# A decoder layer's opening: x and the first weights on two DMA queues, x a second time by rows, one raw buffer set

## The chip, the cores and the metric

The kernel runs on one core of a Trainium2 chip. The metric is the device time of one execution in microseconds, from the first instruction to the last. TensorE multiplies matrices, VectorE (DVE in the profile), ScalarE (ACT) and GpSimd (POOL) work on rows of 128 partitions, and SyncE (SP) issues DMA transfers, which 16 DMA engines carry out. Each engine takes its own instructions strictly in order, and waits for others by semaphores. So an instruction that waits also holds up everything behind it on its engine.

## What the kernel computes

One layer of a decoder with 256 tokens of 1024 channels. Cut to its outline:

```python
h = rmsnorm(x, norm1_g)
proj = h @ w_in                          # 13 groups of columns: kv_c, kv_s, kv_w, q_a, gates, q_b, k_b, v_b ...
q_a, k_s, k_w, q_b, k_b = rope(rmsnorm per head)
y_a = nsa_mixer(...)                     # compressed, selected and window attention, gated
y_b = dilated_mixer(...)
mixed = sigmoid(g_ma) * (y_a @ w_o_a) + sigmoid(g_mb) * (y_b @ w_o_b)
x = x + mixed @ w_out
x = x + square(relu(rmsnorm(x, norm2_g) @ w_up)) @ w_down
```

All arithmetic is float32. The kernel holds each factor of a dense product as two parts, hi (x rounded to the float32r type) and lo (x - hi), and forms hi hi + lo hi + hi lo.

## The kernel before, in words

**Weights.** A list of pieces of [128 partitions, 768 columns] (840 for the four pieces of kv_w) is gone through in the order of use. `load_to` issues the load of a piece into a buffer `raw` (L160 to L164). `split_to` makes the hi part by a ScalarE cast (`wh`, L180) and the lo part by a subtraction (`wl`, L183), on VectorE mostly and on GpSimd for each third piece from the sixth on. `raw` has two buffer sets: one of five for 768 columns, and another (`rawg`) for kv_w alone. A load must wait until the piece that held its buffer has been split.

**The opening.** x lies transposed in `xT`, loaded in four parts that alternate with the four pieces of kv_c. `scale_x` (L242) multiplies by the norm's gain and makes the two parts of h, one on ScalarE (L243), the other on VectorE (L244). The division by the rms is put off to the products' outputs: `proj` (L277) scales each output row by `rs` when it copies it out of the accumulator (`y`, L302). `setup` (L252) works `rs` out: squares on ScalarE (`sx`), three additions on GpSimd, four one-column products on TensorE, then a power of -0.5 on GpSimd (L265). After it come the rotation tables `ropeg`, ten multiplications on GpSimd (L270) that need the loads `rope` and `gr`, and one for the compressed keys (L274).

**What follows.** kv_c's outputs are transposed on TensorE (`tp`, L378) and put into `kvT`; `make_blk` adds position terms on GpSimd (`b32`, L394, four additions), casts on ScalarE (`blk`, L398) and subtracts on VectorE (L399). The projections kv_s, kv_w and q_a run on TensorE in the meantime, then the compression (`hacc`).

**The order.** The kernel's own planner (`Order`) sets products between tasks; after it, a scheduler places each engine's instructions by its own estimate of when they are ready. Eight DMAs can be on their way: the ninth waits for the first, and so on. Any change at the beginning can therefore move instructions far behind it.

Of the kernel before, what the change touches and what calls it, by code (L numbers as in the profile page):

```python
# [11 lines left out]
F32 = mybir.dt.float32  # L12
# [7 lines left out]
S = 256  # L20
# [11 lines left out]
# Steps of tensor-engine time between the stages of a task, and numbers of buffers.  # L32
D = {"qk": 1.0, "sm": 4, "pv": 0.6, "dqk": 3, "dsm": 4, "rope": 8, "turn": 0.3, "kvc": 0.8, "cz": 1, "ch": 1, "ck": 6,
     "most": 3, "warm": 10, "kneed": "nsa4", "pool_lo": 3, "ahead": 5, "extra": 18, "xm": 5, "xn": 3,
# [70 lines left out]
def hybrid_layer(ctx: ExitStack, tc: tile.TileContext, A, out):  # L105
# [50 lines left out]
    def load_to(n):  # L156
        while len(raws) < min(n, len(pieces)):
            src = pieces[len(raws)]
            n = src.shape[1]
            raw = raw_p.tile([128, n], F32, name="raw", tag="raw" if n <= PIECE else "rawg")  # L160
            if len(raws) < 4:
                q = len(raws)
                nc.sync.dma_start(xT[:, 2 * q:2 * q + 2], A["xT"][:, 2 * q:2 * q + 2])
            nc.sync.dma_start(raw[:, :src.shape[1]], src)  # L164
            raws.append(raw)

    def split_to(n):
        most = min(n, len(pieces))
        while len(parts) < most:
# [10 lines left out]
            nc.scalar.copy(hi[:, :m], src)  # L180
# [14 lines left out]
    def cell():  # L195
        """The next [128, 128] block of the stream of blocks."""
# [7 lines left out]
    ident = const.tile([128, 128], F32, name="ident")  # L204
    nc.sync.dma_start(ident, A["ident"])
    g12 = const.tile([128, 16], F32, name="g12")
    nc.sync.dma_start(g12, A["g12"])
    xT = once([128, 8, S], F32, "xT")
    load_to(4)
# [24 lines left out]
    # keep the tensor engine's clock up while the first loads arrive  # L234
# [4 lines left out]
    # hidden state (times its gain, not yet over its rms) in two parts  # L239
    hT = [once([128, 8, S], F32R, f"hT{i}") for i in range(2)]  # L240

    def scale_x(k):  # L242
        nc.scalar.activation(hT[0][:, k], xT[:, k], AF.Copy, scale=g12[:, k:k + 1])  # L243
        nc.vector.scalar_tensor_tensor(hT[1][:, k], xT[:, k], g12[:, k:k + 1], f(hT[0][:, k]),  # L244
                                       op0=OP.mult, op1=OP.subtract)

# [1 line left out]
    rs = const.tile([128, NT], F32, name="rs")  # L248
    idr = const.tile([128, 128], F32R, name="idr")
    ropeg = {}  # L250

    def setup():  # L252
        sx = [once([128, 2, S], F32, f"sx{i}") for i in range(4)]
        for i in range(4):
            nc.scalar.activation(sx[i], xT[:, 2 * i:2 * i + 2], AF.Square, scale=1.0 / 32.0)
            if i:
                nc.gpsimd.tensor_add(sx[0], sx[0], sx[i])
        pt = tp_bank()
        for t in range(NT):
            for k in range(2):  # L260
                nc.tensor.matmul(pt[:, t:t + 1], sx[0][:, k, t * 128:(t + 1) * 128], ones[:, 0:1],
                                 start=k == 0, stop=k == 1)
        ss = const.tile([128, NT], F32, name="ss")
        nc.vector.tensor_scalar(ss, pt[:, 0:NT], EPS, None, op0=OP.add)
        nc.gpsimd.tensor_tensor(rs, ss, nhalf[:, 0:NT], op=OP.pow)  # L265
# [769 lines left out]
```

## Time and profile before

| | us |
|---|---|
| median of three runs | 474.08 (473.75 to 474.11) |
| span of the profiled execution | 474.4 |
| TensorE busy | 452.3 (95%) |
| VectorE busy | 351.9 (74%) |
| ScalarE busy | 295.0 (62%) |
| GpSimd busy | 209.0 (44%) |

The profiled execution's span lies 0.3 us above the median of the timed runs; the profile shows no time of its own outside the span. TensorE's share of 95% is an average: nearly all of its idle time lies in the first 77 us and in four short places later. A row of a timeline gives start and duration in us, engine, line, operation, the tiles written and read with their shapes, how many were merged into the row, and in brackets the idle time before it and what ended it.

### The profile page before, as it was taken

How to read it: one execution, taken by the hardware profiler on the slowest of the kernel's cores; microseconds unless marked ns; L12 is line 12 of the kernel's file. 1: busy time of each engine (PE TensorE's matmuls, PEld its weight loads, DVE VectorE, ACT ScalarE, POOL GpSimd, SP SyncE). 2: the span in 40 equal slices, each digit the busy share in tenths (PEclk: the TensorE clock that was granted, in tenths of full speed). 3: DMA queues.
4: the chain of work that ended last, by engine and by line, in shares of the span. 5: the costliest groups of instructions: out<-in, count | busy, mean ns of one | idle time of the engine just before them, and what ended most of it. 6: DMA issues, size and time to landing. Idle time of an engine off the chain costs nothing.

```text
span 474.4 us, 9304 instructions
## 1 busy us (share of the span) xinstructions
PE 452.3 (95%) x3472; PEld 436.4 (92%) x3474; DVE 351.9 (74%) x572; ACT 295.0 (62%) x637; POOL 209.0 (44%) x203
## 2 busy tenths in 40 slices
PE   7997897999899999999999899999999999999996
PEld 6896777999798898989999899999999999999996
DVE  3959998989988999998557979956556555555450
ACT  5747678487867897858697454665656643433430
POOL 2797775779587782813043519523333310000000
PEclk8999899999899999999999999999999999999999
DMA  7973557563343144234336574777666767767720
GB/s 246 356 232 101 161 170 249 152 193 101 99 140 129 34 134 134 77 103 123 102 96 188 182 225 133 205 199 194 180 192 178 195 194 203 193 205 197 196 87 11
DMA packets 29630, 76.93 MB, mean 162 GB/s; under 512 B 3809, under 2 KB 5265, under 8 KB 29457
## 3 DMA queue, kind: packets, MB, share of 16 engines
q1 hardware_dynamic: 29584, 76.34, 54.5%
q8 instruction: 27, 0.44, 0.4%
q14 instruction: 19, 0.15, 0.1%
HBM read 75.28 MB, written 1.05 MB: 161 GB/s over the span
## 4 chain that ended last, share of the span: by engine, by line
PE 79%; DVE 10%; issue 4%; DMA 3%; ACT 2%; SPq 1%; POOL 0%; DVEq 0%; ACTq 0%; POOLq 0%
PE acc L745 18%; PE acc L746 18%; PE acc L744 18%; PE acc L295 4%; PE acc L296 4%; PE acc L294 4%; DVE wl L183 3%; PE tp L511 2%; DMA raw<-in_kv_c 2%; DMA gr<-in_gr 2%; PE tp L335 1%; PE dsp L693 1%; PE sp L552 1%; DVE t L329 1%; DVE h L873 1%
## 5 line engine op out<-in xcount | busy, mean ns | idle before, releaser
L183 DVE TENSOR_TENSOR wl<-raw,wh 128x768 fp32r<-128x768 f32 (+2 forms) x154 | 160.7, 1047 | 70.5 <-ACT wh L180 69.8
L180 ACT CAST wh<-raw 128x768 fp32r<-128x768 f32 (+2 forms) x183 | 152.1, 841 | 77.8 <-PE acc L745 66.2
L183 POOL TENSOR_TENSOR wl<-raw,wh 128x768 fp32r<-128x768 f32 (+1 forms) x29 | 56.2, 1937 | 62.5 <-ACT wh L180 35.8
L745 PE MATMUL acc<-h,wh 128*128 128x256 f32 x256 | 71.8, 281 | 0.7 <-DVE h L873 0.6
L745 PE MATMUL acc<-u,wh 128*128 128x256 f32 x256 | 71.6, 280 | 0.0
L746 PE MATMUL acc<-u,wl 128*128 128x256 f32 x256 | 71.6, 280 | 0.0
L744 PE MATMUL acc<-u,wh 128*128 128x256 f32 x256 | 71.6, 279 | 0.0
L746 PE MATMUL acc<-h,wl 128*128 128x256 f32 x256 | 71.3, 279 | 0.0
L744 PE MATMUL acc<-h,wh 128*128 128x256 f32 x256 | 71.3, 280 | 0.0
L295 PE MATMUL acc<-wl,hT 128*128 128x384 f32 (+1 forms) x176 | 63.0, 358 | 5.3 <-POOL wl L183 3.2
L294 PE MATMUL acc<-wh,hT 128*128 128x384 f32 (+1 forms) x176 | 60.3, 355 | 2.7 <-ACT wh L180 2.6
L296 PE MATMUL acc<-wh,hT 128*128 128x384 f32 (+1 forms) x176 | 61.1, 350 | 0.0
L911 POOL TENSOR_TENSOR r<-r 128x256 f32<-128x256 f32 x32 | 31.7, 992 | 54.1 <-ACT r L910 54.1
L745 PEld LDWEIGHTS acc<-h,wh 128*128 128x128 f32 x256 | 48.2, 188 | 1.2 <-DVE h L873 1.1
L746 PEld LDWEIGHTS acc<-u,wl 128*128 128x128 f32 x256 | 48.2, 188 | 0.0
L745 PEld LDWEIGHTS acc<-u,wh 128*128 128x128 f32 x256 | 48.2, 188 | 0.0
L744 PEld LDWEIGHTS acc<-u,wh 128*128 128x128 f32 x256 | 48.2, 188 | 0.0
L746 PEld LDWEIGHTS acc<-h,wl 128*128 128x128 f32 x256 | 48.1, 188 | 0.0
L744 PEld LDWEIGHTS acc<-h,wh 128*128 128x128 f32 x256 | 48.0, 188 | 0.0
L295 PEld LDWEIGHTS acc<-wl,hT 128*128 128x128 f32 x176 | 34.7, 197 | 7.3 <-POOL wl L183 3.7
L294 PEld LDWEIGHTS acc<-wh,hT 128*128 128x128 f32 x176 | 33.6, 194 | 4.1 <-ACT wh L180 3.5
L746 PE MATMUL acc<-hT,wl 128*128 128x256 f32 x128 | 37.0, 289 | 0.0
(195 smaller groups left out, 1094.7 us busy)
## 6 DMA issues: line engine op xcount, KB each, us to landing
raw<-in_cells SPq DMA_DIRECT2D x128, 384.0 KB, 3.4
raw<-in_cw SPq DMA_DIRECT2D x10, 384.0 KB, 3.7
raw<-in_q_a SPq DMA_DIRECT2D x8, 384.0 KB, 3.2
raw<-in_q_b SPq DMA_DIRECT2D x8, 384.0 KB, 3.6
raw<-in_k_b SPq DMA_DIRECT2D x8, 384.0 KB, 3.1
raw<-in_v_b SPq DMA_DIRECT2D x8, 384.0 KB, 3.2
raw<-in_kv_w SPq DMA_DIRECT2D x4, 420.0 KB, 8.3
raw<-in_kv_c SPq DMA_DIRECT2D x4, 384.0 KB, 7.0
```

Of the source, the lines that this page charges most:

```text
L180: nc.scalar.copy(hi[:, :m], src)
L183: eng.tensor_sub(lo[:, :m], src, f(hi[:, :m]))
L294: nc.tensor.matmul(o, hT[0][:, k, ts], hi[:, c], start=k == 0, stop=False)
L295: nc.tensor.matmul(o, hT[0][:, k, ts], lo[:, c], start=False, stop=False)
L296: nc.tensor.matmul(o, hT[1][:, k, ts], hi[:, c], start=False, stop=k == 7)
L329: nc.vector.tensor_mul(v, v, st[:, 1, :h][:, :, None].to_broadcast([128, h, 64]))
L335: nc.tensor.transpose(pt[:, i * 128:(i + 1) * 128], src[:, i].rearrange("p a d -> p (a d)"), idr)
L511: nc.tensor.transpose(pt[0:rows, i * 128:(i + 1) * 128], s, ident)
L744: nc.tensor.matmul(o, hi, a[0][k], start=start, stop=False)
L745: nc.tensor.matmul(o, hi, a[1][k], start=False, stop=False)
L746: nc.tensor.matmul(o, lo, a[0][k], start=False, stop=stop)
L911: nc.gpsimd.tensor_mul(r, r, r)
```

## The change

- x with both norms' gains in front of it is one input `xg`, loaded in four tiles; the first holds the gains, which were a load of their own.
- The first two weight pieces are issued by ScalarE on its own DMA queue, the rest by SyncE.
- The first piece's hi part is made on VectorE instead of ScalarE.
- x is loaded a second time by rows (`xrow`, 1 MB in two halves). ScalarE squares each half with a running sum per row, so the GpSimd additions and the one-column products go.
- All pieces share one raw buffer set of five with 840 columns; `rawg` is gone.
- The first 12 products take hi parts first and the lo part last; 12 warm-up products instead of 10.
- The second norm's gains are copied to `g2` on GpSimd. The other removed lines are comments.

```diff
@@ load_to
-            raw = raw_p.tile([128, n], F32, name="raw", tag="raw" if n <= PIECE else "rawg")
-            if len(raws) < 4:
-                q = len(raws)
-                nc.sync.dma_start(xT[:, 2 * q:2 * q + 2], A["xT"][:, 2 * q:2 * q + 2])
-            nc.sync.dma_start(raw[:, :src.shape[1]], src)
+            raw = raw_p.tile([128, 840], F32, name="raw", tag="raw")
+            q = len(raws)
+            if q < 4:
+                nc.sync.dma_start(xg[q], A["xg"][:, q * 512 + 16 * (q > 0):(q + 1) * 512 + 16])
+            (nc.scalar if q < 2 else nc.sync).dma_start(raw[:, :src.shape[1]], src)
+            if q == 3:
+                for t in range(NT):
+                    nc.sync.dma_start(xrow[:, t], A["xrow"][:, t])
@@ split_to
-            nc.scalar.copy(hi[:, :m], src)
+            if n:
+                nc.scalar.copy(hi[:, :m], src)
+            else:
+                nc.vector.tensor_copy(hi[:, :m], src)
@@ setup
-        sx = [once([128, 2, S], F32, f"sx{i}") for i in range(4)]
-        for i in range(4):
-            nc.scalar.activation(sx[i], xT[:, 2 * i:2 * i + 2], AF.Square, scale=1.0 / 32.0)
-            if i:
-                nc.gpsimd.tensor_add(sx[0], sx[0], sx[i])
-        pt = tp_bank()
...
-        nc.vector.tensor_scalar(ss, pt[:, 0:NT], EPS, None, op0=OP.add)
+            nc.scalar.activation(sx, xrow[:, t], AF.Square, scale=1.0 / 32.0, accum_out=ss[:, t:t + 1])
+        nc.vector.tensor_scalar(ss, ss, EPS, None, op0=OP.add)
         nc.gpsimd.tensor_tensor(rs, ss, nhalf[:, 0:NT], op=OP.pow)
+        nc.gpsimd.tensor_copy(g2, xg[0][:, 8:16])
@@ proj
+            if first and i == 0:
+                for h, w in ((0, hi), (1, hi), (0, lo)):
+                    for k in range(2):
+                        for t in range(NT):
+                            nc.tensor.matmul(acc[t][:, :n], hT[h][:, k, t * 128:(t + 1) * 128],
+                                             w[:, k * n:(k + 1) * n], start=h == 0 and k == 0 and w is hi, stop=False)
```

The first place is GpSimd from the rms to the compression blocks. `rs` is the power, `ropeg` the rotation tables, `b32` the block additions; of the lo parts, `wl_642` and `wl_698` are the first and last piece of kv_w, `wl_587` the second of kv_s. Before:

```order
L183 TENSOR_TENSOR wl_642<-raw_101,wh_641 128x840
L265 TENSOR_TENSOR rs_484<-ss_531,nhalf_467 128x2
L183 TENSOR_TENSOR wl_587<-raw_95,wh_586 128x768
L270 TENSOR_TENSOR ropeg1_535<-rope_453,gr_451 128x2x64 x2
...
L183 TENSOR_TENSOR wl_698<-raw_107,wh_697 128x840
L274 TENSOR_TENSOR ropeg5_550<-ropec_455,gr_451 48x128
L394 TENSOR_TENSOR b32_667<-kvT_490,posT_457 128x24x15 x2
L394 TENSOR_TENSOR b32_686<-kvT_490,posT_457 128x24x15 x2
L183 TENSOR_TENSOR wl_734<-raw_113,wh_733 128x768
```

Now, with `wl_582` the second of kv_s, `wl_637` and `wl_693` the first and last of kv_w:

```order
L265 TENSOR_TENSOR rs_490<-ss_528,nhalf_471 128x2
L271 TENSOR_TENSOR ropeg1_536<-rope_457,gr_455 128x2x64 x2
...
L189 TENSOR_TENSOR wl_582<-raw_97,wh_581 128x768
L275 TENSOR_TENSOR ropeg5_551<-ropec_459,gr_455 48x128
L405 TENSOR_TENSOR b32_662<-kvT_497,posT_461 128x24x15 x2
L405 TENSOR_TENSOR b32_681<-kvT_497,posT_461 128x24x15 x2
L189 TENSOR_TENSOR wl_637<-raw_103,wh_636 128x840
L189 TENSOR_TENSOR wl_693<-raw_109,wh_692 128x840
```

All three lo parts stood ahead of the block additions; now one stands behind the ten tables, and two behind the additions.

The second place is TensorE after the transposes of kv_c's first output. `acc_639` and `acc_640` are kv_s's accumulators, `acc_795` is kv_w's. Before:

```order
L294 MATMUL acc_639<-wh_586,hT0_482 128x384
L294 MATMUL acc_640<-wh_586,hT0_482 128x384
L378 MATMUL tp_630<-ident_76,y_620 64x128 x3
L378 MATMUL tp_655<-ident_76,y_620 64x128 x3
L294 MATMUL acc_795<-wh_641,hT0_482 128x420
L295 MATMUL acc_795<-wl_642,hT0_482 128x420
```

Now, with `acc_634` and `acc_635` for kv_s:

```order
L305 MATMUL acc_634<-wh_577,hT0_488 128x384
L305 MATMUL acc_635<-wh_577,hT0_488 128x384
L389 MATMUL tp_625<-ident_453,y_615 64x128 x3
L389 MATMUL tp_650<-ident_453,y_615 64x128 x3
...
L305 MATMUL acc_634<-wh_581,hT0_488 128x384
L305 MATMUL acc_635<-wh_581,hT0_488 128x384
L306 MATMUL acc_634<-wl_582,hT0_488 128x384
```

The transposes, which need `rs`, stand after two products of kv_s instead of after 14, and the first product with `wl_582` follows with no kv_w work ahead of it.

The third place is VectorE around the subtraction of the first block (`blk0`). Before:

```order
L183 TENSOR_TENSOR wl_694<-raw_105,wh_693 128x840
...
L383 COPY kvT_490<-tp_661 64x3x64
L383 COPY kvT_490<-tp_680 64x3x64
L183 TENSOR_TENSOR wl_714<-raw_109,wh_713 128x768
L183 TENSOR_TENSOR wl_718<-raw_111,wh_717 128x768
L399 TENSOR_TENSOR blk0_671<-b32_667,blk0_671 128x16x48
```

Now:

```order
L410 TENSOR_TENSOR blk0_666<-b32_662,blk0_666 128x16x48
L189 TENSOR_TENSOR wl_689<-raw_107,wh_688 128x840
L410 TENSOR_TENSOR blk1_685<-b32_681,blk1_685 128x16x48
L189 TENSOR_TENSOR wl_709<-raw_111,wh_708 128x768
L189 TENSOR_TENSOR wl_713<-raw_113,wh_712 128x768
```

Three lo parts (the third piece of kv_w, the first of q_a and of the compression's weights) have gone from ahead of the subtraction to behind it.

## Rows read from the trace of the kernel before

**Rows 1.** Stretches: us, then busy us of PE, PEld, DVE, ACT, POOL; clock; DMA; GB/s

```profile
0.00:7.00 7.00, 4.15 (x21) 3.96 (x22) 1.31 (x4) 3.43 (x5) 1.88 (x11) 1.00 0.55 176
7.00:15.00 8.00, 6.75 (x28) 5.79 (x28) 5.42 (x8) 6.23 (x12) 3.73 (x3) 0.79 1.02 375
...
44.00:56.00 12.00, 7.75 (x39) 6.87 (x40) 11.95 (x30) 5.64 (x14) 9.80 (x12) 0.86 0.57 173
...
64.00:77.00 13.00, 9.35 (x59) 7.59 (x57) 12.79 (x13) 8.42 (x17) 9.31 (x6) 1.00 0.70 201
77.00:123.00 46.00, 46.00 (x319) 43.79 (x318) 42.43 (x83) 33.72 (x92) 34.42 (x31) 1.00 0.52 156
```

**Rows 2.** Timeline of the opening, all engines

```profile
0.73 0.39 SPq L163 DMA_DIRECT2D xT<-in_xT  x1
...
1.03 3.88 PE L237 MATMUL acc<-ones 128*128 128x128 f32 x20 [1.03 <-POOL ones L232]
...
1.64 0.42 SPq L164 DMA_DIRECT2D raw<-in_kv_c  x1
...
6.73 0.62 PE L294 MATMUL acc<-wh,hT 128*128 128x384 f32 x2 [1.82 <-ACT wh L180]
```

**Rows 3.** The chain that ended last, in order of time, 3 to 24 us

```profile
4.01 8.01 DMA raw<-in_kv_c
...
12.04 7.75 DMA gr<-in_gr
...
20.04 1.52 POOL rs L265
```

**Rows 4.** What the DMA engines moved in 0 to 40 us, per us

```profile
GB/s 0 27 176 163 374 259 234 260 330 343 386 422 409 421 425 401 404 390 404 386 249 230 313 209 353 355 345 104 264 197 267 181 329 273 6 0 0 0 0 0
```

**Rows 5.** Timeline of ScalarE: casts of weights, then the copy of an output

```profile
16.51 3.22 ACT L180 CAST wh<-raw 128x840 fp32r<-128x840 f32 x4 [0.55 <-DVE hT L244]
21.58 0.58 ACT L302 ACTIVATE y<-acc,rs 128x384 f32<-128x384 f32 x1 [1.84 <-POOL rs L265]
```

**Rows 6.** Timeline of GpSimd

```profile
21.52 1.82 POOL L183 TENSOR_TENSOR wl<-raw,wh 128x768 fp32r<-128x768 f32 x1
23.30 7.99 POOL L270 TENSOR_TENSOR ropeg<-rope,gr 128x128 f32<-128x128 f32 x10
31.25 1.99 POOL L183 TENSOR_TENSOR wl<-raw,wh 128x840 fp32r<-128x840 f32 x1
33.19 0.45 POOL L274 TENSOR_TENSOR ropeg<-ropec,gr 48x128 f32<-48x128 f32 x1
33.61 3.99 POOL L394 TENSOR_TENSOR b<-kvT,posT 128x360 f32<-128x360 f32 x4
37.56 1.85 POOL L183 TENSOR_TENSOR wl<-raw,wh 128x768 fp32r<-128x768 f32 x1
```

**Rows 7.** Timeline of VectorE

```profile
28.87 2.10 DVE L183 TENSOR_TENSOR wl<-raw,wh 128x768 fp32r<-128x768 f32 x2 [0.38 <-ACT wh L180]
36.49 3.74 DVE L399 TENSOR_TENSOR blk<-b,blk 128x768 fp32r<-128x768 f32 x1 [5.52 <-ACT blk L398]
...
41.68 0.94 DVE L399 TENSOR_TENSOR blk<-b,blk 128x768 fp32r<-128x768 f32 x1
```

**Rows 8.** Timeline of TensorE: transposes, then the end of kv_w

```profile
22.21 0.85 PE L378 MATMUL tp<-ident,y 128*64 128x128 f32 x6
...
38.40 0.35 PE L296 MATMUL acc<-wh,hT 128*128 128x420 f32 x1
38.59 0.34 PE L294 MATMUL acc<-wh,hT 128*128 128x384 f32 x1
38.76 0.34 PE L295 MATMUL acc<-wl,hT 128*128 128x384 f32 x1
...
46.56 0.44 PE L295 MATMUL acc<-wl,hT 128*128 128x384 f32 x1 [2.67 <-POOL wl L183]
```

**Rows 9.** Whom SyncE's queue waited for in 0 to 45 us: us, times, longest

```profile
SPq L164 <- DVE wl L183: 15.9, 5, 9.9
```

More of the change, by code (lines that the diff above doesn't have):

```diff
@@ L33 @@
 D = {"qk": 1.0, "sm": 4, "pv": 0.6, "dqk": 3, "dsm": 4, "rope": 8, "turn": 0.3, "kvc": 0.8, "cz": 1, "ch": 1, "ck": 6,
-     "most": 3, "warm": 10, "kneed": "nsa4", "pool_lo": 3, "ahead": 5, "extra": 18, "xm": 5, "xn": 3,
+     "most": 3, "warm": 12, "kneed": "nsa4", "pool_lo": 3, "ahead": 5, "extra": 18, "xm": 5, "xn": 3,
      "rbufs": 5, "wbufs": 5, "xb": 3, "phib": 4, "Pb": 4, "yb": 4, "sqb": 2, "t2b": 1, "t1b": 2, "qkb": 4,
@@ L201, in cell @@
         return [w[:, c:c + 128] for w in left[1]]
+    xg = [once([128, 528 if q == 0 else 512], F32, f"xg{q}") for q in range(4)]
+    xT = [xg[k // 2][:, 16 * (k < 2) + k % 2 * S:16 * (k < 2) + k % 2 * S + S] for k in range(8)]
+    xrow = once([128, NT, D_MODEL], F32, "xrow")
+    load_to(4)
     ident = const.tile([128, 128], F32, name="ident")
     nc.sync.dma_start(ident, A["ident"])
[L206 to L209, printed above, removed]
     gr = once([128, 2, 6, 64], F32, "gr")
@@ L242, in scale_x @@
     def scale_x(k):
-        nc.scalar.activation(hT[0][:, k], xT[:, k], AF.Copy, scale=g12[:, k:k + 1])
-        nc.vector.scalar_tensor_tensor(hT[1][:, k], xT[:, k], g12[:, k:k + 1], f(hT[0][:, k]),
-                                       op0=OP.mult, op1=OP.subtract)
+        g = xg[0][:, k:k + 1]
+        nc.scalar.activation(hT[0][:, k], xT[k], AF.Copy, scale=g)
+        nc.vector.scalar_tensor_tensor(hT[1][:, k], xT[k], g, f(hT[0][:, k]), op0=OP.mult, op1=OP.subtract)
     rs = const.tile([128, NT], F32, name="rs")
+    g2 = const.tile([128, 8], F32, name="g2")
     idr = const.tile([128, 128], F32R, name="idr")
@@ L252, in setup @@
     def setup():
-        sx = [once([128, 2, S], F32, f"sx{i}") for i in range(4)]
-        for i in range(4):
-            nc.scalar.activation(sx[i], xT[:, 2 * i:2 * i + 2], AF.Square, scale=1.0 / 32.0)
-            if i:
-                nc.gpsimd.tensor_add(sx[0], sx[0], sx[i])
-        pt = tp_bank()
-        for t in range(NT):
[L260 to L263, printed above, removed]
-        nc.vector.tensor_scalar(ss, pt[:, 0:NT], EPS, None, op0=OP.add)
+        ss = const.tile([128, NT], F32, name="ss")
+        sx = once([128, D_MODEL], F32, "sx")
+        for t in range(NT):
+            nc.scalar.activation(sx, xrow[:, t], AF.Square, scale=1.0 / 32.0, accum_out=ss[:, t:t + 1])
+        nc.vector.tensor_scalar(ss, ss, EPS, None, op0=OP.add)
         nc.gpsimd.tensor_tensor(rs, ss, nhalf[:, 0:NT], op=OP.pow)
+        nc.gpsimd.tensor_copy(g2, xg[0][:, 8:16])
         nc.vector.tensor_copy(idr, ident)
@@ L287, in proj @@
                 scale_x(2 * i + 3)
+            if first and i == 0:
[4 more added lines that the diff above has]
+                                             w[:, k * n:(k + 1) * n], start=h == 0 and k == 0 and w is hi, stop=False)
+                pe(12 * n / 2200)
+                yield 0
             for t in range(NT):
@@ L290, in proj @@
                 ts = slice(t * 128, (t + 1) * 128)
+                if first and i == 0:
+                    continue
                 for kk in range(2):
@@ L971, in _layout @@
     x = a["x"][0]
-    d["xT"] = x.T.reshape(8, 128, S).transpose(1, 0, 2)
-    d["g12"] = np.concatenate([a["norm1_g"][0].reshape(8, 128).T, a["norm2_g"][0].reshape(8, 128).T], 1)
+    d["xg"] = np.concatenate([a["norm1_g"][0].reshape(8, 128).T, a["norm2_g"][0].reshape(8, 128).T,
+                              x.T.reshape(8, 128, S).transpose(1, 0, 2).reshape(128, 8 * S)], 1)
+    d["xrow"] = x.reshape(NT, 128, D_MODEL).transpose(1, 0, 2)
     rows = [a[n][0] for n in ("q_norm_a", "k_norm_slc", "k_norm_win", "q_norm_b", "k_norm_b", "k_norm_cmp")]
```

6 lines of the change are left out of this document (3 added, 3 removed).

## The prediction

> **What bounds the kernel now.** I read the table of stretches first, since the 95% busy of TensorE is an average. From 77 us to 123 us TensorE has no idle time at all, and VectorE is busy for 42.4 of 46 us [rows 1]. Whatever the change gains or loses at the beginning has to show before 77 us. There TensorE is idle for 2.9 us in the first 7, 1.3 us up to 15, 4.3 us between 44 and 56 and 3.7 us between 64 and 77. In two stretches the granted clock is below 1: 0.79 over 8 us and 0.86 over 12 us, each worth 1.7 us of full clock [rows 1], a piece of time at 1.2 instead of 2.4 GHz.
>
> Next I asked what ends TensorE's waits after 37 us. The longest is 2.67 us, for a lo part on GpSimd [rows 8]. VectorE is idle for 5.52 us until 36.49, because the subtraction of the first block waits for GpSimd's block additions, and then runs almost without a gap: 11.95 of 12 us from 44 us on, 12.79 of 13 from 64 us [rows 1, 7]. So from 36.5 us to 77 us VectorE is the bound, and what starts it is a GpSimd chain: the power `rs`, ten rotation tables of 7.99 us together, a lo part, four block additions of 3.99 us [rows 3, 6]. The chain of waits leads further back to the load of `gr` and the third kv_c piece [rows 3]. The opening matters mainly through that chain.
>
> **When `rs` and the tables come.** The third kv_c piece lands at 4.01 + 8.01 = 12.0 us [rows 3], with 1992 KB issued up to it (three parts of x, three pieces, gains, `ident`). Now it is 1928 KB: 11.9 us. Up to the second half of `xrow` come another 256 + 384 + 1024 = 1664 KB; at about 410 GB/s, which rows 4 show from 11 us to 19 us, that takes 4.1 us: 16.0 us. ScalarE squares 1024 columns; a cast of 840 takes 3.22/4 = 0.81 us [rows 5], so about 1.0 us, an estimate by columns. With 0.2 us for the small VectorE step and 1.52 us for the power [rows 3], `rs` is there at 18.7 us, against 21.6 us before. `gr` waits for the same piece before it is issued, with 2240 KB ahead of it instead of 2668 KB: 11.9 + 7.75 - 1.05 = 18.6 us [rows 3, 4]. The tables begin at 18.7 us instead of 23.30: 4.6 us earlier. That is the gain of the change, and I take it as whole.
>
> **What two queues bring.** The first weight piece is issued at 0.73 us instead of 1.64 [rows 2], a gain of 0.9 us at most if bandwidth is shared; the gain is zero where DMA engines are full. From below the bound is a loss: the first part of x shares its engines with 768 KB of weights. From above, had the first 7 us a DMA share of 1.00 in place of 0.55 from 1.75 us on (rows 4 have nothing before the second us), all loads would come about 1.4 us earlier [rows 1, 4]. I take 0 and keep -1.4 and +1 for the range. The Trainium skill ("DMA: Bandwidth & Descriptors", "Issuing engines are not separate DMA queues") says that DMAs of all issuing engines share the same 16 DMA engines, so that a second one saves issue time only. By that rule the value is the 0.9 us of the issue rows for one piece and none for the total of bytes; no run here shows two queues yet.
>
> The edits around the first products cost little. VectorE casts the first piece between its own scalings: about 1 us in place of ScalarE's 0.8, in a gap of 1.82 us that ends with that cast [rows 2]. Two more warm-up products (0.39 us each, 3.88/10) fill the same gap. If it stays open the clock falls as it does now. The four one-column products and the additions on GpSimd go; nothing waits for that. `g2` is eight columns on an engine that waits anyway.
>
> **What TensorE loses.** kv_c's last piece lands 1.6 us after its third, at 13.5 us; cast 0.8, lo part 1.05 [rows 7], 12 products of 0.17 us (starts in rows 8): kv_c is done at 17.4 us. Then the transposes stand after two products of kv_s, and need `rs` and an output copy of 0.58 us [rows 5]: a wait of about 1.5 us, until 19.3 us, which the kernel before does not have, since it holds 14 products there.
>
> The larger wait follows. Counted from `rs`, TensorE does copy 0.6, transposes 0.85, ten products 1.7, transposes 0.85, two products 0.3 and stands at the second kv_s lo part at `rs` + 4.3 us. That lo part is behind the ten tables: `rs` + 7.99 + 1.82 = `rs` + 9.8 us [rows 6]. So TensorE waits 5.5 us, whenever the loads come, from 23.0 us to 28.5 us. After a pause of that length I expect the clock to fall as in the other two places, 1.7 us more. Behind it: 34 products of kv_s, two of kv_w, and the first kv_w lo part, ready at 28.5 + 0.45 + 3.99 + 1.99 = 34.9 us, just in time; 46 products at 0.19 us. kv_w ends at 43.7 us, 45.4 with the clock, against 38.59 before [rows 8]: 6.8 us later. What the kernel before loses from 44 us to 56 us, 4.25 us idle and 1.7 us of clock [rows 1], comes off, if TensorE then runs through. There remain 0.9 us.
>
> **What VectorE loses.** Its subtraction of the first block took 3.74 us, and its twin 0.94 [rows 7]. It began at 36.49 and ended 0.8 us after GpSimd's lo part, which ran from 37.56 us to 39.4: it was held while GpSimd worked. Now the block additions end at 33.0 us, but two lo parts of 1.99 us follow at once [rows 6]: VectorE is free at 37.0 us instead of 39.4, 2.4 us earlier. It owes three lo parts of its own that were done ahead, 1.05 us each, and will be held once more by the lo part of 1.85 us that was inside the old hold: 3.15 + 1.85 - 2.4 = 2.6 us later.
>
> The Trainium skill ("GPSIMD Engine Reference", "Specifications") says that GpSimd shares its SBUF interfaces with VectorE's instructions of two SBUF inputs. The 3.74 us agree; two lo parts beside the tables, 2.10 us together [rows 7], do not show it, so by the rows I charge the hold to lo parts and block additions, not to tables.
>
> The one raw set is the last term. Even before, SyncE's weight loads waited 15.9 us in five waits for VectorE's lo parts [rows 9], without TensorE having waited for a load there. With four buffers fewer the loads of q_a and the compression are issued only as kv_w's lo parts end; about 0 to 1 us, inside VectorE's lateness. I take 0.
>
> **The sum.** TensorE's own account says 0.9 us later, VectorE's 2.6; the ends lie close and each engine waits for the other, so I take the middle, 1.7 us. On the span of 474.4 us that gives 476.1; the timed median lies 0.3 us under the span, so 475.8 us, slower.
>
> **Rivals.** *Faster: the earlier tables pay.* If VectorE's subtraction is not held but begins when its block is there, it starts at about 31.9 us, 4.6 us earlier, and owes 3.15 us: 1.4 us ahead. TensorE's account without the fall of the clock is 0.9 - 1.7 = 0.8 us ahead. For it: the lo parts beside the tables ran unhindered. Against it: the 3.74 us. It decides if the first subtraction takes about 1 us. Time 474.1 - 1.4 = 472.7; with loads 1.4 us earlier, 471.3.
>
> *No change: the later idle time takes it.* TensorE is idle for 3.65 us from 64 us to 77 us [rows 1]. If its lateness of 0.9 us goes in there, and VectorE's lo parts come in an order that puts urgent ones first, the time stays at 474.1. Against it: VectorE is busy for 12.79 of those 13 us, so what it has late it passes on.
>
> *Slower by more: loads.* If the two queues delay x by 1 us and the raw set costs another, all three terms move: 477.8. I count it with the forecast.
>
> **Chances.** Slower 0.46 (475.8, by itself 474.8 to 478.3), faster 0.31 (472.7), no change 0.23 (474.1). About 0.2% (0.95 us) is what a measurement of this kernel can tell from no change. The range takes in both rivals' ends and the unknown loads: 471.0 to 478.6.
>
> **What would show it.** Right: `rs` near 18.7 us, a TensorE wait of 5 to 6 us for a GpSimd lo part near 23 us, a granted clock under 1 behind it, kv_w's end near 45 us, a first block subtraction of several us. Wrong: `rs` after 20 us (the loads), no such wait (GpSimd's tables shorter), or VectorE's first subtraction of 1 us with TensorE through kv_w by 42 us, which is the faster rival. If all steps hold and the time does not, the balance from 44 us to 77 us was misjudged.

## The result, and the profile after

The changed kernel takes 480.08 us (median of 4 runs, 479.58 to 481.74) against 473.91 us before (4 runs, 473.50 to 474.11), a ratio of 1.0128 with a 95% interval of 1.0105 to 1.0151. It is slower, as forecast, but by 6.2 us instead of 1.7, outside the range. A later series of runs gave 481.65 us for the changed kernel (ratio 1.0127, 1.0101 to 1.0153).

The stretches that answer to [rows 1], with two more from 15 to 31 us; columns as there.

```profile
0.00:7.00 7.00, 4.98 (x25) 4.82 (x25) 1.51 (x4) 2.90 (x5) 2.07 (x12) 1.00 0.74 247
7.00:15.00 8.00, 8.00 (x45) 7.83 (x46) 6.08 (x12) 7.05 (x14) 0.72 (x1) 1.00 1.03 405
15.00:23.00 8.00, 5.26 (x32) 4.54 (x31) 6.56 (x9) 5.29 (x10) 7.93 (x12) 0.96 0.94 333
23.00:31.00 8.00, 8.00 (x39) 7.98 (x39) 6.87 (x2) 5.07 (x7) 8.00 (x7) 0.83 0.36 119
44.00:56.00 12.00, 9.79 (x54) 9.40 (x55) 9.64 (x24) 8.37 (x22) 6.07 (x8) 0.72 0.58 193
77.00:123.00 46.00, 45.50 (x297) 42.42 (x297) 42.43 (x78) 32.59 (x91) 34.28 (x30) 0.96 0.50 155
```

The opening is far better than before: 247 GB/s in the first 7 us, TensorE busy without a gap from 7 to 15 us at a granted clock of 1.00 (0.79 before [rows 1]). From 15 us on this turns: VectorE is at work on two instructions in eight microseconds (23 to 31), the loads fall to 119 GB/s, and the granted clock is below 1 in four of the six stretches.

GpSimd in the changed kernel, to be read against [rows 6].

```profile
14.04 0.72 POOL L265 TENSOR_TENSOR rs<-ss,nhalf 128x2 f32<-128x2 f32 x1 [8.91 <-DVE idr L267]
15.07 5.65 POOL L271 TENSOR_TENSOR ropeg<-rope,gr 128x128 f32<-128x128 f32 x10 [0.32 <-DMA gr<-in_gr]
20.68 1.80 POOL L189 TENSOR_TENSOR wl<-raw,wh 128x768 fp32r<-128x768 f32 x1
23.57 3.90 POOL L405 TENSOR_TENSOR b<-kvT,posT 128x360 f32<-128x360 f32 x4
27.44 3.97 POOL L189 TENSOR_TENSOR wl<-raw,wh 128x840 fp32r<-128x840 f32 x2
36.87 1.09 POOL L332 TENSOR_TENSOR t<-y,ropeg 128x96 f32<-128x96 f32 x2 [5.45 <-ACT y L313]
```

rs is there at 14.76 us, the ten tables take 5.65 us, and all three low parts that GpSimd owes stand behind them, two even behind the block additions. VectorE over the same time, against [rows 7]:

```profile
18.89 1.10 DVE L189 TENSOR_TENSOR wl<-raw,wh 128x768 fp32r<-128x768 f32 x1 [0.66 <-ACT wh L184]
24.42 7.88 DVE L189 TENSOR_TENSOR wl<-raw,wh 128x840 fp32r<-128x840 f32 x1 [1.13 <-ACT wh L184]
32.23 0.95 DVE L410 TENSOR_TENSOR blk<-b,blk 128x768 fp32r<-128x768 f32 x1
33.10 1.02 DVE L189 TENSOR_TENSOR wl<-raw,wh 128x840 fp32r<-128x840 f32 x1
```

A subtraction that takes 1.02 us nine microseconds later is held for 7.88 us: it begins under GpSimd's additions and ends 0.9 us after GpSimd's second low part (27.44 + 3.97 = 31.41). Beside the tables (15.07 to 20.72) VectorE's subtraction was not held (1.10).

What hangs on that subtraction are the loads. SyncE's queue before, then in the changed kernel; the weights of the compression are in_cw:

```profile
22.29 0.33 SPq L164 DMA_DIRECT2D raw<-in_cw  x1
23.37 0.33 SPq L164 DMA_DIRECT2D raw<-in_cw  x1
```

```profile
23.70 0.42 SPq L164 DMA_DIRECT2D raw<-in_q_a  x1
32.34 2.14 SPq L164 DMA_DIRECT2D raw<-in_cw  x2
35.88 0.33 SPq L164 DMA_DIRECT2D raw<-in_q_a  x1
```

With one set of five buffers the first of these loads goes out at 32.34 us, when the held low part frees its buffer; before it went out at 22.29. ScalarE's queue in the changed kernel shows who stands behind it:

```profile
28.58 0.83 ACT L184 CAST wh<-raw 128x768 fp32r<-128x768 f32 x1
35.41 0.84 ACT L184 CAST wh<-raw 128x768 fp32r<-128x768 f32 x1 [6.00 <-DMA raw<-in_cw]
36.15 0.57 ACT L313 ACTIVATE y<-acc,rs 128x384 f32<-128x384 f32 x1
44.20 0.51 ACT L364 CAST kd<-t 128x384 fp32r<-128x384 f32 x1
```

The cast waits 6.00 us for the load, and the copy of kv_s's finished product (y, 36.15) behind it waits along; its rotation on GpSimd begins after 5.45 us without work (36.87), and its key parts kd (44.20) stand behind that. The longest of TensorE's waits in the first 90 us of the changed kernel (us in total, times, longest):

```profile
PE tp L346 <- ACT kd L364: 3.6, 1, 3.6
PE acc L306 <- POOL wl L189: 2.7, 1, 2.7
PE acc L755 <- ACT wh L184: 1.8, 1, 1.8
PE tp L346 <- DVE kd L365: 1.4, 1, 1.4
```

The first profiles of both kernels have the same idle time on TensorE in all (18.3 us); in the changed one more of the work runs at half clock (mean granted clock 0.984 against 0.989). To see where time goes, take the start of the same product, counted from the last one, in both kernels (for before a second profiled execution, span 473.3; the changed kernel's has 477.8). In the first row the changed kernel's product is the 3,432nd from the end, since the eight one-column products of the rms still stand behind this place before, and not in the changed kernel:

| product from the end | before | changed | changed minus before |
|---|---|---|---|
| 3,440 | 11.32 | 9.16 | -2.16 |
| 3,380 | 22.16 | 18.32 | -3.84 |
| 3,320 | 32.32 | 33.12 | +0.80 |
| 3,260 | 47.07 | 49.21 | +2.14 |
| 3,200 | 58.54 | 59.05 | +0.51 |
| 3,140 | 67.91 | 68.47 | +0.55 |
| 3,020 | 85.82 | 88.92 | +3.10 |
| 1,900 | 244.48 | 247.88 | +3.40 |
| 1,500 | 293.76 | 297.26 | +3.50 |
| 100 | 457.71 | 462.12 | +4.41 |

The opening wins 3.8 us. Part of it is clock: the 128x384 products of the opening start 0.32 us apart up to 13.2 us in this execution of before, and 0.18 us apart from 7.2 us on in the changed kernel. By the product that starts at 33 us the lead is gone: 2.70 us of waiting and 3.4 us at half clock. The waits for kd come next, but at 59 us they have left almost nothing, since the kernel before waits in the same place, for a low part ([rows 8], 46.56). What stays is lost between 68 and 89 us. ScalarE, VectorE, GpSimd and SyncE in the changed kernel there, with one row of before (second execution) at the end:

```profile
65.78 2.23 DVE L189 TENSOR_TENSOR wl<-raw,wh 128x768 fp32r<-128x768 f32 x1
68.04 0.33 SPq L164 DMA_DIRECT2D raw<-in_cw  x1
72.09 0.62 ACT L184 CAST wh<-raw 128x512 fp32r<-128x512 f32 x1 [3.01 <-DMA raw<-in_cw]
72.61 0.28 ACT L444 ACTIVATE z<-z 128x96 f32<-128x96 f32 x1
73.20 1.91 POOL L189 TENSOR_TENSOR wl<-raw,wh 128x768 fp32r<-128x768 f32 x1
73.35 1.88 DVE L445 SCALAR_TENSOR_TENSOR z<-z,z 128x96 f32<-128x96 f32 x1
75.45 0.81 ACT L184 CAST wh<-raw 128x768 fp32r<-128x768 f32 x1
```

```profile
71.47 0.24 DVE L434 SCALAR_TENSOR_TENSOR z<-z,z 128x96 f32<-128x96 f32 x1
```

The last load of in_cw goes out when a low part on VectorE ends; its cast waits 3.01 us, and a step of the compression (z) stands behind that cast. VectorE's next step of it then takes 1.88 us beside a low part of GpSimd, against 0.24 before. ScalarE's cast at 75.45 stands behind that too, and for this cast TensorE waits 1.85 us, the 1.8 in the list, with 3.4 us at half clock from 76.9 us on. Over the next 200 us the distance swings, and it ends 0.4 us larger. Then, in the last 160 us, where both kernels issue the same products in the same order without a single wait, it loses another microsecond. The products in 300 to 460 us, first before (second execution), then changed, then changed in a second execution whose span is 482.8; the second number and its count are TensorE's:

```profile
300.00:460.00 160.00, 160.00 (x1372) 159.95 (x1371) 91.46 (x124) 82.51 (x136) 28.98 (x30) 1.00 0.68 188
```

```profile
300.00:460.00 160.00, 160.00 (x1364) 159.94 (x1363) 91.75 (x123) 83.80 (x141) 31.51 (x32) 1.00 0.69 193
```

```profile
300.00:460.00 160.00, 159.87 (x1331) 159.70 (x1330) 90.94 (x122) 82.02 (x139) 31.87 (x33) 1.00 0.68 189
```

At a granted clock of 1.00 in all three, 160 us hold 1,372, 1,364 and 1,331 products of the same shape: a step of 116.6, 117.3 and 120.1 ns from one to the next (busy time over count). Over the last 1,500 products a step of 117.3 costs 1.0 us and one of 120.1 some 5.

### The profile page after: what moved, and what is told of

Its sections match the earlier page's. It is cut to its first block, busy times and chain, and to the rows that moved or that the text cites. A ratio compares the mean times of both kernels' runs of the same rounds, so it can differ in the third digit from the quotient of the medians.

```text
span 477.8 us, 9292 instructions
## 1 busy us (share of the span) xinstructions
PE 455.7 (95%) x3468; PEld 439.7 (92%) x3470; DVE 351.0 (73%) x573; ACT 296.2 (62%) x636; POOL 201.2 (42%) x201
## 4 chain that ended last, share of the span: by engine, by line
PE 70%; DVE 15%; DMA 5%; issue 4%; ACT 4%; POOL 1%; SPq 0%; DVEq 0%; ACTq 0%
PE acc L757 18%; PE acc L756 17%; PE acc L755 17%; PE acc L306 3%; PE acc L305 3%; PE acc L307 3%; DVE wl L189 3%; DMA raw<-in_kv_s 2%; DVE t L335 2%; ACT P L587 2%; PE tp L522 2%; DMA raw<-in_cw 2%; PE tp L346 1%; ACT wh L184 1%; PE dsp L704 1%
## 5 line engine op out<-in xcount | busy, mean ns | idle before, releaser
L189 DVE TENSOR_TENSOR wl<-raw,wh 128x768 fp32r<-128x768 f32 (+1 forms) x154 | 166.3, 1081 | 79.3 <-ACT wh L184 77.3
L184 ACT CAST wh<-raw 128x768 fp32r<-128x768 f32 (+1 forms) x182 | 152.0, 839 | 89.8 <-PE acc L756 68.1
L306 PE MATMUL acc<-wl,hT 128*128 128x384 f32 (+1 forms) x172 | 61.1, 355 | 2.7 <-POOL wl L189 2.7
L307 PE MATMUL acc<-wh,hT 128*128 128x384 f32 (+1 forms) x172 | 60.0, 350 | 0.0
L305 PE MATMUL acc<-wh,hT 128*128 128x384 f32 (+1 forms) x172 | 58.2, 349 | 1.4 <-ACT P L587 1.4
L755 PE MATMUL acc<-hT,wh 128*128 128x256 f32 x128 | 37.9, 296 | 1.8 <-ACT wh L184 1.8
L756 PE MATMUL acc<-hT,wh 128*128 128x256 f32 x128 | 37.4, 292 | 0.0
```

Of the source, the lines that this page charges most:

```text
L189: eng.tensor_sub(lo[:, :m], src, f(hi[:, :m]))
L305: nc.tensor.matmul(o, hT[0][:, k, ts], hi[:, c], start=k == 0, stop=False)
L306: nc.tensor.matmul(o, hT[0][:, k, ts], lo[:, c], start=False, stop=False)
L307: nc.tensor.matmul(o, hT[1][:, k, ts], hi[:, c], start=False, stop=k == 7)
L755: nc.tensor.matmul(o, hi, a[0][k], start=start, stop=False)
L756: nc.tensor.matmul(o, hi, a[1][k], start=False, stop=False)
```

## The experiments

Names used in the expectations: theory L, the one raw set starves the loads; G, the order on GpSimd costs the time, by its low parts behind the tables and by the hold of VectorE; O, the opening itself costs (two queues, x read twice); P, the step of the dense products depends on where tiles lie in SBUF; X, that step falls by chance in each execution.

**Two raw sets again (e1_two_sets).**

```
-            raw = raw_p.tile([128, 840], F32, name="raw", tag="raw")
+            raw = raw_p.tile([128, n], F32, name="raw", tag="raw" if n <= PIECE else "rawg")
```

> The changed kernel with the two raw buffer sets of before (768 and 840 columns, five each); the rest of the change stays. Theory L (one set of five starves the loads: with it the loads for the compression's weights were issued only at 32.3 us, when a low part held up on VectorE gave its buffer free; ScalarE then waited 6.0 us for one of them, and TensorE stood 3.6 and 1.4 us behind the key parts): 472 to 475 us, no wait of ScalarE for a load over 2 us between 30 and 50 us, the loads issued before 28 us. Rival G (GpSimd's position in the order, low parts behind tables and block additions, costs the time): gain only as far as GpSimd's two kv_w low parts move; TensorE's idle at 41 to 47 us is gone if they stand ahead of the tables. Rival O (the opening itself, two queues and x read a second time, costs it): stays at 479 to 480 us.

Measured 485.83 us (1.0229, 1.0202 to 1.0256): slower still, and outside all three ranges. The loads do what L says: in_cw goes out from 23.12 us on, and no cast waits more than 1.2 us for it; GpSimd takes three low parts ahead of the tables; the lead is 2.1 us at product 3,260. But VectorE and TensorE meet the hold later (below, e8), and the step in the end is 120 ns (1,330 products in 300 to 460 us). So the late loads are L's, and undoing them alone buys nothing here.

**One raw set in the kernel before (e2_before_one_set).** The same line, the other way round, in the kernel before.

> The kernel before with one set of five 840-column raw buffers for all pieces and nothing else changed. Theory L: 477 to 481 us, with waits of ScalarE for a load of several us between 25 and 50 us. Rival G: 474 to 476 us, whatever the new order of the low parts costs. Rival O: 474 us, unchanged.

478.58 us (1.0094, 1.006 to 1.0129): the one set alone costs some 4 us, as L said. In the profiled execution 2.4 us of this are there by product 1,500, and 1.0 comes behind it by a step of 117.3 ns (1,364 products in 300 to 460 us); the edit also moves every tile behind the buffers (P, below). The order shows how the front loses: as in the changed kernel, the ten tables now stand ahead of GpSimd's low parts. GpSimd in this run:

```profile
15.73 6.30 POOL L270 TENSOR_TENSOR ropeg<-rope,gr 128x128 f32<-128x128 f32 x10 [0.76 <-DMA raw<-in_kv_s]
25.59 2.31 POOL L183 TENSOR_TENSOR wl<-raw,wh 128x840 fp32r<-128x840 f32 x1 [0.69 <-ACT wh L180]
```

ScalarE waits 3.1 us for a weight load at 41 us and 3.5 at 72 us, and TensorE waits 2.1 us three times before 80 us. The chain of 65 to 80 us is nearly that of the changed kernel: behind the wait of 3.5 us the z step takes 1.88 us on VectorE, and TensorE stands 2.15 us at 76.5 us; the kernel is 0.2 us ahead at product 3,140 and 3.8 behind at 3,020. L and G come together here: in every kernel of this study with one set, unless the low parts are put first by hand, the scheduler fills GpSimd with tables first; with two sets it takes two or three low parts first, where GpSimd has any.

**All loads on one queue (e3_one_queue).**

```
-            (nc.scalar if q < 2 else nc.sync).dma_start(raw[:, :src.shape[1]], src)
+            nc.sync.dma_start(raw[:, :src.shape[1]], src)
```

> The changed kernel with the first two weight loads issued by SyncE again, so that all loads stand on one queue; the order on the compute engines stays the same. Theory L: within 1 us of 480, since the loads that bind come 20 us later; the first product starts 0.3 to 1 us later. Rival O, if the second queue costs: 1 to 5 us faster. If the second queue is what brought the early loads (rs at 14.8 us instead of the 18.7 forecast): rs 1 to 3 us later and the time up to 2 us longer.

481.36 us (1.0134, 1.0107 to 1.0161), not told apart from the changed kernel's 480.08 and 481.65. The first 7 us move 236 GB/s instead of 247, and the squares of x start at 12.18 us instead of 11.26; but the first products start 0.7 us earlier with one queue (the fifth at 7.03 instead of 7.74 us), against what was expected. The second queue is worth nothing that can be measured at the end; O's part about the queue falls.

**No low part on GpSimd before piece 12 (e4_lowparts_vector).**

```
-            eng = nc.gpsimd if p and 4 <= n < POOL_LO_END and n % p == p - 1 else nc.vector
+            eng = nc.gpsimd if p and 12 <= n < POOL_LO_END and n % p == p - 1 else nc.vector
```

> The changed kernel with the first low parts on GpSimd from piece 12 on, not from piece 4 on, so that kv_s's and kv_w's low parts are all VectorE's; one raw set stays. Rival G: 472 to 476 us, since no low part of VectorE is held behind GpSimd's block additions. Theory L in its strict form (five buffers are too few whoever frees them): 477 to 480 us, ScalarE still waits several us for a load between 30 and 45 us.

481.69 us (1.0139, 1.0113 to 1.0165), by the time nearest to L, above its range. The trace says otherwise: the lead is 2.7 us at product 3,320, 3.8 at 3,260, 3.3 at 3,020 and 1.4 at 1,900, so up to there the edit wins 4.8 us on the changed kernel. It is lost at 245 to 270 us, at the end of the dilated attention (TensorE's longest wait in 240 to 270 us):

```profile
PE acc L755 <- ACT yT L556: 2.2, 1, 2.2
```

Behind it the clock is at half for 3.4 us, and from 1,500 on the step is 118.5 ns (1,350 products in 300 to 460 us). G holds for the front; the time is lost twice elsewhere.

The wait for yT is one of order, not of coming early. It is 2.20 us in six kernels: this one, e12, e13 and e14, which reach the place ahead of the kernel before, and e1 and e8, which reach it 3 to 5 us behind. In all six the last product of the dilated attention (dpo) is the 1,779th from the end, and the next one already needs its output. In the kernels before and changed it is the 1,813th and the 1,810th, and TensorE has over fifty products behind it before it waits again.

**Second executions of both kernels (e5_before_again, e6_after_again).** No edit.

> The kernel before, unchanged, for a second profiled execution. Its first profile has a span of 474.4 us, 2 us more than its timed median leaves for a span (472.2). Expected: 472 to 473 us of span; which stretch gets shorter is open. If the dense products' step differs from 116.67 ns in the last 150 us (matmul start to matmul start), the step belongs to the execution; if it stays 116.67 ns, it belongs to the kernel.

474.78 us, ratio 1.0003 (0.9989 to 1.0017), span 473.3, step 116.6 ns again. The first execution of before was a microsecond longer, all of it before product 3,020.

> The changed kernel, unchanged, for a second profiled execution. Theory P (the step of the dense products is a property of where the tiles lie in SBUF): 117.33 ns again in the last 150 us, and 479.5 to 481 us. Rival X (it differs from execution to execution): another step, as 116.67 or 118.67 ns, and a time that goes with it, 1 us for each 0.67 ns.

481.65 us, but the profiled execution is the longest of six (484.6) and has the step 120.1. Its front is behind by 4.4 us at product 1,900, a microsecond more than in the first execution, and the end by 9.2. So P's 117.33 ns fell, and X holds for the changed kernel: its own runs spread from 478.14 to 484.6, and the step is part of that. Before kept its step in both executions.

**The same instructions at other addresses (e7_before_shifted, e15_before_64, e11_after_shifted).** A wider raw buffer, of which as much is used as before, moves every tile that lies behind it in SBUF.

```
-            raw = raw_p.tile([128, n], F32, name="raw", tag="raw" if n <= PIECE else "rawg")
+            raw = raw_p.tile([128, n + 8 * (n <= PIECE)], F32, name="raw", tag="raw" if n <= PIECE else "rawg")
```

(24 in place of 8 for e15_before_64; 856 in place of 840 columns in the changed kernel for e11_after_shifted.)

> The kernel before with its raw buffers of 768 columns made 776 wide, of which 768 are used as before: no instruction changes its place or its size, but every tile of split weights lies at a multiple of 128 bytes in its SBUF partition instead of 96 bytes past one, as in the kernel with the two sets restored (485.83 us). Theory P: the dense products' step rises from 116.67 to about 120 ns and the time to 480 to 484 us. Theory L and G (only waits count): 473.5 to 475 us.

479.50 us (1.0092, 1.0078 to 1.0105), a little under P's range. It is 1.4 us behind at product 1,500 and 4.2 at 100. Its products in 300 to 460 us:

```profile
300.00:460.00 160.00, 160.00 (x1349) 159.95 (x1348) 90.30 (x122) 81.80 (x137) 30.04 (x31) 1.00 0.68 190
```

> The kernel before with its raw buffers of 768 columns made 792 wide: no instruction changes place or size, the split weights lie 64 bytes past a multiple of 128 instead of 96. Theory P (placement sets the step of the dense products): the step in the last 150 us is 116.67 to 120 ns and the time follows it, 1 us for each 0.67 ns over the 474.7 us of 116.67 ns. If only multiples of 128 are slow: 116.67 ns and 474 to 475.5 us.

477.05 us (1.0036, 1.0013 to 1.006), with

```profile
300.00:460.00 160.00, 160.00 (x1359) 159.95 (x1358) 90.36 (x122) 81.97 (x136) 29.59 (x31) 1.00 0.68 189
```

> The changed kernel with raw buffers of 856 instead of 840 columns, of which as many are used as before: no instruction changes place or size, the split weights lie 32 bytes past a multiple of 128 instead of 96. Theory P: the step of the dense products in the last 150 us is this placement's own, 116.67 to 118.67 ns; at 116.67 the time is 477 to 478.5 us, the front's loss alone. Rival X (the step falls by chance in each execution of the changed kernel): 480 to 482 us with the same spread of 6 us as the unshifted kernel.

483.14 us (1.018, 1.0149 to 1.0211), all six between 482.98 and 485.81, with

```profile
300.00:460.00 160.00, 160.00 (x1334) 159.95 (x1333) 90.49 (x122) 81.64 (x139) 31.12 (x32) 1.00 0.68 190
```

For the time P is shown: with every instruction in its place, addresses alone move the kernel before from 474.7 to 477.05 and 479.50 us. For the step it is shown less firmly. It goes along, from 116.6 to 117.7 and 118.6 ns, but each value is from one execution, and the changed kernel's two executions differ by 2.8 ns with no tile moved. e11_after_shifted fits neither theory's range. A rule of 128 bytes does not come out: by the offsets that the expectations give, which no trace here holds, the multiple goes with 118.6 ns, 32 past it with 119.9, and 96 past it with 116.6 before and 117.3 or 120.1 in the changed kernel. Why stays open.

**Two raw sets at other addresses (e8_two_sets_shifted).** e1_two_sets with the 768-column set 792 wide.

> The changed kernel with the two raw sets of before, the 768-column set made 792 wide, so that the split weights lie 96 bytes past a multiple of 128, as in the kernels before and after, and not at the multiple, as in the first run with two sets (485.83 us). Theory P with L: the step falls to 117 to 118.7 ns, the time to 472 to 477 us, faster than the changed kernel. P without L: 478 to 481 us. If P is wrong: 484 to 487 us.

481.84 us (1.0155, 1.0137 to 1.0172), between the ranges, 4 us better than e1_two_sets, with 1,365 products in 300 to 460 us; the scheduler also put VectorE's and ScalarE's instructions in another order in places, so the comparison is not of addresses alone. What remains against before is a hold at 63 us, VectorE's rows first, then GpSimd's:

```profile
63.42 2.14 DVE L338 TENSOR_TENSOR t<-t,t 128x384 f32<-128x384 f32 x1 [1.04 <-POOL t L332]
65.48 2.55 DVE L189 TENSOR_TENSOR wl<-raw,wh 128x768 fp32r<-128x768 f32 x1
```

```profile
63.35 3.87 POOL L189 TENSOR_TENSOR wl<-raw,wh 128x768 fp32r<-128x768 f32 x2
```

An addition that takes 0.56 us elsewhere takes 2.14 and a low part of 0.94 takes 2.55 while GpSimd does its own two; TensorE waits 5.1 us for that low part. The lead of 1.9 us at product 3,260 is 6.4 us behind at 3,140. G again, in another place.

**GpSimd's first low parts put ahead of the tables (e9_low_first).**

```
+            if eng is nc.gpsimd and n < 12:
+                with tc.high_priority():
+                    eng.tensor_sub(lo[:, :m], src, f(hi[:, :m]))
...
```

> The changed kernel with GpSimd's low parts of kv_s and kv_w set at the head of the scheduler's order: on GpSimd the second kv_s low part then stands behind one table instead of eight, and the two kv_w low parts stand apart. Same work on the same engines, one raw set. Theory G: TensorE's wait of 2.7 us at 22.5 us and the half clock behind it (1.7 us of work) go, so the changed kernel's lead at 18 us is still there at 33 us, and the time is 475 to 478 us. Theory L alone: the late loads at 32 to 38 us stay, 479 to 481 us. If the later waits take it back: 479 to 481 us with the lead at 33 us there.

482.65 us (1.0163, 1.0124 to 1.0202), above all ranges: the expectation fell. The kv_s low part is early (17.22 us, behind one table) and the wait at 22 us is gone. But the kv_w low parts cannot start before their casts, and now stand apart, the first behind nine tables and the additions:

```profile
25.55 3.74 POOL L409 TENSOR_TENSOR b<-kvT,posT 128x360 f32<-128x360 f32 x4
29.25 1.96 POOL L191 TENSOR_TENSOR wl<-raw,wh 128x840 fp32r<-128x840 f32 x1
```

TensorE waits 5.2 us for it (26.06 to 31.27), and the lead of 4.0 us becomes a lag of 4.0 between products 3,380 and 3,320. The wait moved down the queue by two pieces and grew.

**The rms as before, x loaded once (e10_old_rms).** The squares go over the four x pieces, with three additions on GpSimd and four small products, and the load at line 167 is gone.

```
-            nc.scalar.activation(sx, xrow[:, t], AF.Square, scale=1.0 / 32.0, accum_out=ss[:, t:t + 1])
+                nc.scalar.activation(sx[i][:, k], xT[2 * i + k], AF.Square, scale=1.0 / 32.0)
+            if i:
+                nc.gpsimd.tensor_add(sx[0], sx[0], sx[i])
...
```

> The changed kernel with its rms taken as before (squares of the four x pieces, three additions on GpSimd, four small products on TensorE), and x not loaded a second time; the two queues, the order of the opening and the one raw set stay. If the second load of x or the new rms costs (rival O): 476 to 478 us. Theory G: GpSimd reaches its low parts still later, since three additions stand ahead of the tables: 480 to 484 us, with TensorE's wait for the second kv_s low part as long or longer than 2.7 us.

478.77 us (1.0082, 1.0051 to 1.0114), some 1.3 to 2.9 us faster than the changed kernel, and not slower as G expected: TensorE waits 3.6 us for VectorE's low parts, but none for GpSimd's. Part of O seems to stand: the new rms costs in this order, though the intervals overlap. It also buys the lead: the thirteenth dense product starts at 9.19 us without it and at 9.16 with it, but behind it TensorE waits 1.6 us at 14.5 us for a low part on VectorE, and the lead is gone at 3,380. A lead that is not kept is worth nothing.

**No early low part on GpSimd in the kernel before (e12_before_lowparts).** The edit of e4_lowparts_vector.

> The kernel before with the first low parts on GpSimd from piece 12 on, not from piece 4 on. Theory G: GpSimd's early low parts cost the kernel before too (a first block subtraction of 3.74 us, TensorE's wait of 2.67 us at 46.6 us): 470 to 473 us, unless it comes back at 245 to 270 us as it did for the changed kernel with the same edit: then 474 to 477 us. Rival: VectorE has no room for three more low parts: over 475 us with waits of TensorE for VectorE's low parts before 40 us.

477.79 us (1.0055, 1.0036 to 1.0074). The front does gain, 4.7 us at product 3,260 and 2.6 at 1,900. Between 1,800 and 1,700 it loses 3.5: the same wait of 2.2 us for yT, 1.1 us more, and 3.4 us at half clock. The rival's time fits as well, but its sign, waits for VectorE's low parts before 40 us, comes to 0.8 us at 14 us.

**The opening alone, and with GpSimd's low parts from piece 12 (e13_opening_alone, e14_opening_lowparts).** The edits of e1_two_sets and e10_old_rms in the changed kernel; then that of e4_lowparts_vector as well.

> The changed kernel with two raw sets and the rms of before: what is left of the change is the opening (x and its gains in four pieces in front, the first two weight loads issued by ScalarE, the order of the first products, two more warm-up products). If the opening alone is a gain, as the changed kernel's lead of 3.6 us at the end of its first 30 products says: 470 to 474 us. If the lead is lost again whatever the order on GpSimd is (it comes back as a wait behind VectorE at 43 to 68 us, as in the two-set run that kept its lead until 49 us): 474 to 478 us. In both cases TensorE waits less than 1 us at 22 us, since GpSimd takes its low parts ahead of the tables.

478.17 us (1.0059, 1.0039 to 1.0079). The lead goes early: the squares of x, four pairs of 0.71 us, now stand between the first casts on ScalarE, so TensorE waits 2.0 us at 10 us with half clock behind it, and product 3,380 starts at 23.38 us, 1.2 behind. (The "lead of 3.6 us" in the expectation set two different products side by side; it was 2.2.) The kernel leads by 2.6 us at 3,260 and 1.1 at 1,900, and then

```profile
PE acc L759 <- ACT yT L560: 2.2, 1, 2.2
PE acc L760 <- DVE mT L883: 1.3, 1, 1.3
```

> The same as the opening alone, and GpSimd's low parts start with piece 12 instead of piece 4. If GpSimd's early low parts are what takes the lead back: 469 to 473 us, faster than the kernel before. If the lead is taken back at 245 to 270 us, where VectorE and ScalarE end the dilated attention, as with the same edit in the other two kernels: 474 to 478 us.

476.88 us (1.0039, 1.0021 to 1.0057), the best of the kernels with the new opening, with 1.6 us of lead at product 1,900 and 2.7 us given back at 245 to 270 us. None beat the kernel before. The raw sets alone are what e13_opening_alone and e10_old_rms differ by: 478.17 us with two, 478.77 with one, which is no clear difference.

## Why the prediction was right or wrong

**The direction and the first link.** That the changed opening brings the tables ahead of GpSimd's low part of kv_s, that TensorE then waits for it and loses clock, was right, and is the largest loss in the table: 4.6 us between products 3,380 and 3,320. The wait was put at 5.5 us and is 2.70 (3.4 in the second execution); ten tables take 5.65 us instead of the 7.99 of [rows 6], and why is open (VectorE is busy for 4.6 us beside them against 7.7 before, but in e2_before_one_set they take 6.30 with 3.1). The half clock was put at 1.7 us of work, and that was right: 22.30 to 25.71 us ran at half.

**The opening was priced too low.** rs was forecast for 18.7 us and came at 14.76, tables for 18.7 and began at 15.07. The two queues were taken as 0, which e3_one_queue bears out at the end of the kernel; what was missed is that x and the weights in front of everything else fill the DMA engines from the start (247 GB/s against 176 in [rows 1]) and that the first products then run on without a gap at a granted clock of 1.00: 3.8 us of lead at 18 us. By the Trainium skill ("DMA: Bandwidth & Descriptors", "Issuing engines are not separate DMA queues") a second issuing engine saves only the time it takes to issue, since all share the same 16 DMA engines; the runs agree, 236 GB/s with one and 247 with two in the first 7 us.

**The hold was right, its place wrong.** VectorE was to be held in its block subtraction until GpSimd's kv_w low parts end; it was held 7.88 us in a low part of its own, and the first block subtraction took 0.95 us. kv_w's products were to end at 43.7 to 45.4 us and end at 39.4, because the 3.8 us of lead stood against it. A short subtraction and kv_w done before 42 us were named as the signs of the faster rival. Both came, and the kernel was slower: they did not see a hold in another instruction.

**TensorE's account came out by luck.** It put the kernel 0.9 us behind at 56 us, as 6.8 us lost by kv_w's end less the losses of 44 to 56 us, 5.95 us together, that were to come off. Measured, kv_w ends 0.8 us later (39.4 against 38.6), little comes off (in these 12 us TensorE is idle for 2.2 us and the granted clock is 0.72), and product 3,200 at 59 us is 0.5 behind.

**The step that failed is the one raw set, taken as 0 (0 to 1 us).** It alone costs the kernel before some 4 us (e2_before_one_set), 2.4 of them before product 1,500. It does so in two ways that the prediction had apart and did not bring together: it lets the scheduler put the tables first, and it makes the next loads wait for low parts that GpSimd holds up. The prediction followed the buffers only to the loads' issue, not to the cast that waits for the load and to the y behind that cast. This is the 6.00 us on ScalarE, the 3.6 and 1.4 us before kd, and the half clock at 46 to 53 us, which is why the losses of 44 to 56 us did not come off; and it is the chain of 65 to 80 us, which leaves 2.6 us. What runs show of it is e2 and these chains. An undo does not show it: with two sets again (e1, e8, and e13 against e10) nothing clear is gained; in e1 and e8 the new order holds VectorE in other places, at 63 us in e8. So the price of the one set in the changed kernel itself stays open.

**One term was not in the sum at all**: the step of the dense products, 0.9 us of the 4.5 in the changed kernel's first execution and 4.9 of the 9.5 in its second. No row before shows it, since a busy TensorE at clock 1.00 looks the same at 116.6 and at 120.1 ns; only counting products does. That the changed kernel's placement gives it is not shown; that placement moves the time of the kernel before is.

Together, for the first execution of the changed kernel against the second of before: -3.8 (opening), +4.6 (wait and clock at 19 to 33 us), -0.3 (33 to 68 us), +2.6 (the chain behind the last in_cw load, with its clock), +0.4 (89 to 294 us), +0.9 (step) = 4.4 us, the difference of the two spans (4.5); the timed 6.2 lies between this and the second execution's 9.5. The sum's last term, 0.3 us from span to timed median, was misread: a timed run is 1.8 us longer than its span (475.14 and 473.3, 479.58 and 477.8), so the first profile of before was of a run some 2 us above the median. The forecast of the difference does not hang on it.

The rival "slower by more: loads" had its time (477.8) nearer to the result, and its half on the raw set is what is seen on ScalarE (x came earlier, not later); it was carried as part of the forecast and priced too low.

**Left open.** Why the step takes its values, and what makes the scheduler leave the end of the dilated attention without other products (e1, e4, e8, e12, e13, e14). The parts do not add up: one set alone +4, opening alone +3.4, all together +6.2; each brings an order of its own.

## What to carry to other kernels

Where a scheduler sets the order, the price of a smaller buffer set is read in three places in turn: what moves ahead on the engines that now seem free, which release the next loads wait for, and what stands behind the instruction that waits for the load. A lead won in the opening is worth nothing until it is followed to the next place where two engines meet. Before comparing two kernels within one per cent, count equal products in an equal stretch without waits: if the counts differ, part of the difference is not the change's.

## What the runs showed of the hardware

- The same 128x256 products, without waits and at a granted clock of 1.00, ran at 116.6, 117.3, 117.7, 118.6, 119.9 and 120.1 ns from start to start in the mean, steady through 150 us of one execution. The kernel before kept its value in two executions, the changed kernel had two values in two; with tiles moved in SBUF, and nothing else, the kernel before had others (474.7, 477.05 and 479.50 us).
- GpSimd's block additions and 840-column subtractions held one VectorE subtraction of two SBUF operands for 7.88 us (1.02 alone), through six GpSimd instructions in a row, and one low part a VectorE step of 96 columns for 1.88 us (0.24). Its table products, two operands as well, one of them a broadcast, did not (1.08 to 1.10 beside them).
- A second issuing engine for the first two weight loads moved 247 instead of 236 GB/s in the first 7 us; the time did not show it.
